# Full-array and paired-head products in the mixers of a hybrid encoder step

## The chip, the cores and the metric

The kernel runs on one core of a Trainium2 chip. The metric is the device time of one launch in microseconds, as the median of repeated runs. Five engines work side by side, each with its own in-order queue: TensorE (PE, matrix products; its weight loads are listed as PEld), VectorE (DVE), ScalarE (ACT), GpSimd (POOL) and SyncE (SP, which here only issues DMAs). A scheduler (the Tile framework) fixes the order of each queue when the program is built.

## What is computed

One layer of a streaming encoder, for a prompt of 2048 tokens and a sample chunk of 64 tokens with a past of 2048. Model width is 1024, and four mixers have four heads of 64 columns each.

```
proj = x @ w_in                                  # split among the mixers
A gated delta rule, chunks of c tokens, state S (64 x 64 per head):
   lm  = strictly lower part of (beta k) k^T * decay
   sol = (I + lm)^-1 [beta v, beta k exp(g)];  v_new = u - w S
   o   = (q exp(g)) S + (q k^T * decay) v_new;  S = S exp(g_last) + (k decay)^T v_new
B stick-breaking attention: z = q k^T / 8, weights from log-sigmoids and a running sum over keys
C mLSTM: o = (a_prev q C + (q k^T * D) v) / den;  C, n = decayed + (w k)^T [v, 1]
D HGRN2: a[t,s] = sum_k q[t,k] k[s,k] exp(l[t,k] - l[s,k]);  o = (q exp(l)) S + a v;  S likewise
o = rmsnorm per head, gates;  x = LN(alpha x + o @ w_out);  x = LN(alpha x + relu(x @ w1 + b1)^2 @ w2 + b2)
```

## The kernel before

The prompt is cut into 16 tiles of 128 tokens, two tiles make a unit (8 units, and one more for the 64 sample tokens), four tiles make a block (4 blocks). For each block the program projects the tokens, runs the attention over all key tiles up to the block, and then runs the mixers unit by unit: `gates`, `gdn`, `mlstm`, `hgrn`. The output product (`mix`) and the MLP of a block follow later in the program. The scheduler interleaves all of it: between the small products of the mixers, TensorE's queue holds products of the projections and of the MLP.

The large products (L413 to L415, L466) split each operand into a high and a low part in float32r and add three products; they use all 128 rows and 128 columns of the array. Their weights come through a ring of buffers `whi` and `wlo` (W_SP of each), loaded by DMAs that SP issues in order with all others (`move`, L192). The mixers' products are plain float32. A float32 product is issued as two instructions, so the counts of a row are twice the number of calls; a transpose is one.

An operand that occupies only part of the partitions makes a product on a part of the array. In the profile a row says so by two numbers, rows*columns: `128*128` is the full array, `64*128` uses 64 rows (partitions of the operands), `128*64` fills 64 columns (partitions of the result).

The places that the change touches:

- `attention`, L1197 to L1205: for each key tile and head a score product of keys (high part in one half of the partitions, low part in the other, `kk`) with the high part of the queries `qs` over 128 rows (L1204), then a second one of the 64 rows of the keys' high part with the queries' low part `ql` (L1205). There are 160 such pairs: four blocks, four heads, 4, 8, 12 and 16 key tiles. L1163/L1164 and L1211/L1212 are the attention's other products, on the full array.
- `gdn`, the inverse of the delta rule's matrix: the loop over the unit's tiles `j` at L872 inverts one tile's matrix after the other, by products on 64 x 64 parts of the array (L889, L894, L906, L911) and transposes (L900), each waiting for a copy on ScalarE or a subtraction on VectorE. Then L924/L925 multiply by the inverse: for each head, first a 64*64 product for the upper half, then a 128*64 one for the lower half.
- State updates, L937 (delta rule), L1007 (mLSTM), L1132 (HGRN2): for each head a product with 64 columns, into the half of the partitions that the head has in the state.
- `mlstm`, L982 to L986: the scores of the heads 0 and 2, then those of 1 and 3, each over the 64 rows of that half, through one PSUM buffer (ring `h`, one bank).
- `hgrn`, L1088 to L1112: for each head products of 32 columns at five levels (L1105, 64*32), and of 64 and 32 columns (L1100, 64*64 and 64*32), then copies on ScalarE and a multiplication and a reduction on VectorE, again through the one bank of ring `h`.
- The buffer rings at the head of the file (L25 to L36).

Of the kernel before, what the change touches and what calls it, by code (L numbers as in the profile page):

```python
# [13 lines left out]
P = 128  # L14
# [10 lines left out]
W_RAW, W_SP = 4, 7  # L25
R_X2 = 7
MIX_AT = (8, 12)
R_AS, R_AR, R_AQ, R_AK, R_OB = 4, 4, 2, 4, 1
# [7 lines left out]
R_G2, R_G1, R_H2, R_H1 = 7, 12, 2, 12  # L36
# [17 lines left out]
def encoder_step(ctx: ExitStack, tc: tile.TileContext, a, o):  # L54
# [139 lines left out]
    def rows(i):  # L194
        return slice(64 * i, 64 * i + 64)
# [567 lines left out]
    def gdn(u):  # L763
# [102 lines left out]
        for j in range(n):  # L866
            for d, s in ((sq.wd[j], wb), (sq.wtd[j], tb)):
                for h in range(4):
                    r0 = (j * 4 + h) * NB
                    SP.dma_start(diag(d, h, half), s[r0 : r0 + NB])  # L870
        for j in range(n):
            c, t = ch[j], u.tiles[j]  # L872
            sl = slice(j * C, (j + 1) * C)
            c.W, c.WT = g1([C, 4, half]), g1([C, 4, half])
            for d, dst in ((sq.wd[j], c.W), (sq.wtd[j], c.WT)):
                for x in range(2):
                    d0 = x * (half * 4 * half + half)
                    SP.dma_start(dst[x * half : x * half + half], d[d0 : d0 + half * 4 * half].rearrange("(r h c) -> r h c", r=half, h=4))

            bs = 16  # L880
            while 2 * bs < C:
                cu, yt = g1([C, 4, half]), g1([C, 4, half])
                for x in (A, B):
                    m0 = x.start % 64
                    POOL.tensor_tensor(cu[x], c.U[x, :, x], bmask[bs][x, m0 : m0 + half].unsqueeze(1).to_broadcast([half, 4, half]), ALU.mult)
                py = ps([C, 4, half])
                for h in range(4):
                    for x in (A, B):
                        PE.matmul(py[x, h, :], lhsT=cu[x, h, :], rhs=c.WT[x, h, :], start=True, stop=True)  # L889
                ACT.copy(yt, py)  # L890
                p1 = ps([C, 4, half])
                for h in range(4):
                    for x in (A, B):
                        PE.matmul(p1[x, h, :], lhsT=yt[x, h, :], rhs=c.W[x, h, :], start=True, stop=True)  # L894
                DVE.tensor_tensor(c.W, c.W, p1, ALU.subtract)

                m = C if 4 * bs < C else half
                p2 = ps([half, 4, m])
                for h in range(4):
                    PE.transpose(p2[:, h, :], c.W[:m, h, :], ident[:m, :m])  # L900
                for x in (A, B)[: m // half]:
                    ACT.copy(c.WT[x], p2[:, :, x])
                bs *= 2
            py = ps([C, 4, half])
            for h in range(4):
                PE.matmul(py[B, h, :], lhsT=c.U[A, h, B], rhs=c.WT[A, h, :], start=True, stop=True)  # L906
            yt = g1([C, 4, half])
            ACT.copy(yt[B], py[B])
            p1 = ps([half, 4, half])
            for h in range(4):  # L910
                PE.matmul(p1[:, h, :], lhsT=yt[B, h, :], rhs=c.W[B, h, :], start=True, stop=True)  # L911
            c.WB = g1([C, 4, half])
            POOL.tensor_copy(c.WB[B], c.W[B])
            ACT.mul(c.WB[A], p1, -1.0)

# [19 lines left out]
            sd = ps([P, 2, 64])  # L935
            for h in range(4):
                PE.matmul(sd[rows(h % 2), h // 2, :], lhsT=c.kd[:, h, :], rhs=vn[:, h, :], start=True, stop=True)  # L937
            for h in range(4):
                r = rows(h % 2)
                DVE.scalar_tensor_tensor(S[r, h // 2, r], S[r, h // 2, r], c.dec[r, h // 2 : h // 2 + 1], sd[r, h // 2, :], ALU.mult, ALU.add)  # L940
# [8 lines left out]
    def mlstm(u):  # L949
        C, n, N, b, sq = u.C, u.n, u.N, u.b, u.seq  # L950
        Cn = sq.Cn
        for j in range(n):
            t = u.tiles[j]
            q = h1([P, 2, C])
            SP.dma_start(q, b.mlq[:, :, t.off : t.off + C].rearrange("g p t -> p g t"))
            k = h1([C, 4, 64])
# [48 lines left out]
            sd = ph([P, 2, 65])  # L1005
            for h in range(4):
                PE.matmul(sd[rows(h % 2), h // 2, :], lhsT=kw[:, h, :], rhs=v[:, h, :], start=True, stop=True)  # L1007
            for h in range(4):
                i = h % 2
                r = rows(i)  # L1010
                cs = Cn[r, h // 2, 65 * i : 65 * i + 65]
                DVE.scalar_tensor_tensor(cs, cs, app[r, h // 2, C - 1 : C], sd[r, h // 2, :], ALU.mult, ALU.add)


    def hgrn(u):
# [10 lines left out]
        for t in u.tiles:  # L1026
# [61 lines left out]
            for g in range(2):  # L1088
# [480 lines left out]
```

## Time and profile before

| what | value |
|---|---|
| time, median of 3 runs | 3481.16 us (3478.19 to 3486.56) |
| time of the profiled execution | 3476.89 us |
| span of its instructions | 3475.2 us |
| TensorE busy | 3298.9 us, 95% |
| VectorE busy | 2265.2 us, 65% |
| ScalarE, GpSimd busy | 1376.5 us (40%), 850.8 us (24%) |
| mean granted TensorE clock | 0.957 |

The page gives busy time by engine, the span in 40 slices, the chain of work that ended last, and the costliest groups of instructions. A timeline row gives the start in us, the length, engine, line, operation, what it writes and reads, and a count where neighbours are merged. Lengths of products overlap, since they are pipelined: what a product costs the queue is the distance from its start to the start of the next one.

### The profile page before, as it was taken

What the parts mean: (1) busy time and instruction counts of PE and PEld (TensorE: products, weight loads), DVE (VectorE), ACT (ScalarE), POOL (GpSimd) and SP (SyncE); (2) the same over time, 40 slices, a digit from 0 to 9 for tenths busy, and PEclk for the clock granted to TensorE, in tenths of its full rate; (3) what the DMA queues carried; (4) which work ended last, traced back from release to release, by engine and by line L of the source; (5) the groups of instructions that cost most, each with busy time, mean ns of one, the idle gap of its engine ahead of it and who ended that gap; (6) DMA issues with size and microseconds to landing.
All of it is one profiled execution on the core that took longest, in us unless ns stands there. A gap on an engine that the chain in (4) does not pass through costs nothing.

```text
span 3475.2 us, 61244 instructions
## 1 busy us (share of the span) xinstructions
PE 3298.9 (95%) x21186; PEld 2702.3 (78%) x21186; DVE 2265.2 (65%) x5524; ACT 1376.5 (40%) x3308; POOL 850.8 (24%) x907
## 2 busy tenths in 40 slices
PE   7988999899989999999999999999999999999997
PEld 7987787878776777777677767777777778798986
DVE  2327647547767897669968985797686354564445
ACT  2224434434545455555555544445242111121111
POOL 4322212211124234443525322133021000010001
PEclk9998898899988998999999989999999999999999
DMA  7995665466565786668769555574866587675552
GB/s 226 306 328 170 188 194 189 140 209 186 182 194 192 255 273 218 217 228 256 250 197 308 185 175 161 183 243 146 286 210 208 164 291 234 230 227 164 164 163 77
DMA packets 575313, 731.44 MB, mean 210 GB/s; under 512 B 104680, under 2 KB 305308, under 8 KB 575004
## 3 DMA queue, kind: packets, MB, share of 16 engines
q1 hardware_dynamic: 575004, 727.53, 65.0%
q8 instruction: 168, 2.75, 0.3%
q14 instruction: 141, 1.16, 0.1%
HBM read 544.37 MB, written 182.94 MB: 209 GB/s over the span
## 4 chain that ended last, share of the span: by engine, by line
PE 59%; DVE 12%; DMA 5%; issue 2%; SPq 1%; ACT 1%; POOL 1%; POOLq 0%; DVEq 0%; ACTq 0%
PE d L413 16%; PE d L415 15%; PE d L414 15%; PE a L1205 1%; PE d L466 1%; PE po L1212 1%; PE po L1211 1%; PE a L1164 1%; DVE acc L1426 1%; PE a L1163 1%; DMA vv<-x 1%; PE a L1204 1%; DMA x<-x1d 1%; PE h L1105 1%; DVE ar L1169 1%
## 5 line engine op out<-in xcount | busy, mean ns | idle before, releaser
L413 PE MATMUL d<-XH,whi 128*128 128x512 f32 (+1 forms) x1840 | 666.1, 363 | 9.4 <-ACT whi L405 4.0
L414 PE MATMUL d<-XL,whi 128*128 128x512 f32 (+1 forms) x1840 | 665.4, 362 | 2.0 <-DVE XL L429 2.0
L415 PE MATMUL d<-XH,wlo 128*128 128x512 f32 (+1 forms) x1840 | 660.8, 360 | 0.3 <-POOL wlo L406 0.3
L1426 DVE TENSOR_TENSOR acc<-d,acc 128x512 f32<-128x512 f32 x564 | 385.0, 687 | 188.0 <-PE d L415 177.2
L413 PE MATMUL d<-whi,hh 128*128 128x512 f32 x992 | 403.6, 407 | 11.3 <-DVE acc L1426 9.5
L1161 POOL TENSOR_TENSOR ar<-as,ar 128x512 fp32r<-128x512 f32 (+3 forms) x177 | 208.9, 1180 | 786.5 <-ACT ar L1160 675.0
L415 PE MATMUL d<-whi,hh 128*128 128x512 f32 x992 | 397.0, 400 | 0.0
L413 PEld LDWEIGHTS d<-XH,whi 128*128 128x128 f32 x1840 | 349.7, 190 | 60.0 <-ACT whi L405 4.2
L414 PE MATMUL d<-wlo,hh 128*128 128x512 f32 x992 | 395.5, 399 | 0.0
L414 PEld LDWEIGHTS d<-XL,whi 128*128 128x128 f32 x1840 | 349.6, 190 | 52.1 <-issue 3.4
L415 PEld LDWEIGHTS d<-XH,wlo 128*128 128x128 f32 x1840 | 349.7, 190 | 49.0 <-issue 2.3
L406 POOL TENSOR_TENSOR wlo<-raw,whi 128x512 fp32r<-128x512 f32 (+1 forms) x204 | 276.8, 1364 | 334.1 <-ACT whi L405 198.6
L413 PE MATMUL d<-whi,XH 128*128 128x256 f32 (+1 forms) x1024 | 295.2, 296 | 5.9 <-DVE x L528 4.3
L414 PE MATMUL d<-wlo,XH 128*128 128x256 f32 (+1 forms) x1024 | 298.4, 293 | 1.1 <-DMA wlo<-wsp 1.1
L415 PE MATMUL d<-whi,XL 128*128 128x256 f32 (+1 forms) x1024 | 297.8, 293 | 0.0
L1405 ACT ACTIVATE x<-d,cbig 128x512 f32<-128x512 f32 (+1 forms) x160 | 97.8, 611 | 474.3 <-PE d L415 466.9
L1407 DVE CAST hh<-x 128x512 fp32r<-128x512 f32 (+1 forms) x160 | 80.2, 501 | 255.3 <-ACT x L1406 254.9
L413 PEld LDWEIGHTS d<-whi,hh 128*128 128x128 f32 x992 | 188.9, 190 | 58.3 <-DVE acc L1426 11.9
L415 PEld LDWEIGHTS d<-whi,hh 128*128 128x128 f32 x992 | 188.7, 190 | 45.6 <-issue 1.9
L414 PEld LDWEIGHTS d<-wlo,hh 128*128 128x128 f32 x992 | 189.1, 191 | 40.8 <-issue 0.5
L413 PEld LDWEIGHTS d<-whi,XH 128*128 128x128 f32 x1024 | 198.2, 197 | 10.3 <-ACT whi L405 4.5
L414 PEld LDWEIGHTS d<-wlo,XH 128*128 128x128 f32 x1024 | 201.2, 197 | 5.0 <-DMA wlo<-wsp 1.8
(444 smaller groups left out, 6542.7 us busy)
## 6 DMA issues: line engine op xcount, KB each, us to landing
whi<-wsp SPq DMA_DIRECT2D x644, 256.0 KB
wlo<-wsp SPq DMA_DIRECT2D x644, 256.0 KB
wsp<-whi SPq DMA_DIRECT2D x196, 256.0 KB
wsp<-wlo SPq DMA_DIRECT2D x196, 256.0 KB
raw<-in_w_dram SPq DMA_DIRECT2D x128, 256.0 KB
raw<-in_w_in_dram SPq DMA_DIRECT2D x52, 256.0 KB
ak<-kk SPq DMA_DIRECT2D x80, 128.0 KB
ak<-vv SPq DMA_DIRECT2D x80, 128.0 KB
```

Of the source, the lines that this page charges most:

```text
L406: POOL.tensor_tensor(lo, raw, hi.bitcast(F32), ALU.subtract)
L413: PE.matmul(out, lhsT=lh, rhs=rh, start=start, stop=False)
L414: PE.matmul(out, lhsT=lh, rhs=rl, start=False, stop=False)
L415: PE.matmul(out, lhsT=ll, rhs=rh, start=False, stop=stop)
L466: PE.matmul(pt, lhsT=lhs(k), rhs=r, start=k == ks[0] and i == 0, stop=k == ks[-1] and i == 1)
L1105: PE.matmul(pc[32 * qd : 32 * qd + 32, 32 * li : 32 * li + 32], lhsT=lh[r, ts_], rhs=rh[r, ts_], start=True, stop=True)
L1161: POOL.tensor_tensor(sl, sp, sh.bitcast(F32), ALU.subtract)
L1163: PE.matmul(c, lhsT=tri_, rhs=sh, start=True, stop=False)
L1164: PE.matmul(c, lhsT=tri_, rhs=sl, start=False, stop=True)
L1405: ACT.activation(r, pt, AF.Relu, bias=b1c(ff))
L1407: DVE.tensor_copy(h[:, f, cs], r)
L1426: lambda pt, first, acc=acc: DVE.tensor_tensor(acc, pt, acc, ALU.add),
```

## The change

Buffers are moved between the rings: W_SP 7 to 6, the staging ring `x2` 7 to 6, `aq` 2 to 3, `g2` 7 to 10, `g1` 12 to 9, `h2` 2 to 3.

- Attention: `ql` is loaded for each head into both halves of the partitions (two DMAs a head instead of one for two heads), and the second score product runs over 128 rows. It then also adds the product of the two low parts.
- Delta rule: both tiles' inverses are made side by side, each step for both tiles before the next step; one copy and one subtraction serve both. The inverse is put together in one array WF of 128 x 128 for each head (a memset and two copies on GpSimd, one scaling on ScalarE), and the product with it is one product of the full array for each head.
- mLSTM: a second copy of the queries `qw` with zeros in the other head's half (a memset on GpSimd, two DMAs) lets one product over 128 rows make the scores of two heads; one VectorE operation for all four heads.
- HGRN2: two heads share one PSUM bank; the products of 64 columns are cut into two of 32; copies, multiplication and reduction serve two heads.
- State updates: one product of the full array for two heads; of its result the two diagonal blocks are read.

```diff
-W_RAW, W_SP = 4, 7
-R_X2 = 7
+W_RAW, W_SP = 4, 6
+R_X2 = 6
...
-R_AS, R_AR, R_AQ, R_AK, R_OB = 4, 4, 2, 4, 1
+R_AS, R_AR, R_AQ, R_AK, R_OB = 4, 4, 3, 4, 1
...
-R_G2, R_G1, R_H2, R_H1 = 7, 12, 2, 12
+R_G2, R_G1, R_H2, R_H1 = 10, 9, 3, 12
...
+        while 2 * bs < C:
+            cu, yt = g2([C, n, 4, half]), g2([C, n, 4, half])
...
+            py = ps([C, n, 4, half])
+            for j in range(n):
+                for h in range(4):
+                    for x in (A, B):
+                        PE.matmul(py[x, j, h, :], lhsT=cu[x, j, h, :], rhs=WT[x, j, h, :], start=True, stop=True)
+            ACT.copy(yt, py)
...
+            DVE.tensor_tensor(W, W, p1, ALU.subtract)
...
+        for j in range(n):
+            WF = ch[j].WF = g2([C, 4, C])
+            POOL.memset(WF[B, :, A], 0.0)
+            POOL.tensor_copy(WF[A, :, A], W[A, j])
+            POOL.tensor_copy(WF[B, :, B], W[B, j])
+            ACT.mul(WF[A, :, B], p1[:, j], -1.0)
...
-                PE.matmul(pv[A, h, :], lhsT=c.W[A, h, :], rhs=R[A, h, :], start=True, stop=True)
-                PE.matmul(pv[B, h, :], lhsT=c.WB[:, h, :], rhs=R[:, h, :], start=True, stop=True)
+                PE.matmul(pv[:, h, :], lhsT=c.WF[:, h, :], rhs=R[:, h, :], start=True, stop=True)
...
-            sd = ps([P, 2, 64])
-            for h in range(4):
-                PE.matmul(sd[rows(h % 2), h // 2, :], lhsT=c.kd[:, h, :], rhs=vn[:, h, :], start=True, stop=True)
+            sd = ps([P, 2, P])
+            for g in range(2):
+                PE.matmul(sd[:, g, :], lhsT=pairs(c.kd)[:, g, :], rhs=pairs(vn)[:, g, :], start=True, stop=True)
...
+            qw = h2([P, 2, 2 * C]).rearrange("p g (i t) -> p g i t", i=2)
+            POOL.memset(qw, 0.0)
+            for i in range(2):
+                SP.dma_start(qw[rows(i), :, i, :], b.mlq[:, rows(i), t.off : t.off + C].rearrange("g p t -> p g t"))
...
-            for i in range(2):
-                r = rows(i)
-                pq = ph([C, 2, C])
-                for g in range(2):
-                    PE.matmul(pq[:, g, :], lhsT=kT[r, g, :], rhs=q[r, g, :], start=True, stop=True)
-                DVE.scalar_tensor_tensor(E[:, i::2, :], pq, 0.125, E[:, i::2, :], ALU.mult, ALU.mult)
+            pq = ph([C, 4, C])
+            for g in range(2):
+                PE.matmul(pq[:, 2 * g : 2 * g + 2, :], lhsT=kT[:, g, :], rhs=qw[:, g], start=True, stop=True)
+            DVE.scalar_tensor_tensor(E, pq, 0.125, E, ALU.mult, ALU.mult)
...
+            for i in range(2):
+                r = rows(i)
+                pc = ph([C, 2, 256])
+                for g in range(2):
...
+                            for c in range(0, x, 32):
+                                PE.matmul(pc[d0 + c : d0 + c + 32, g, 192 : 192 + x], lhsT=F[x][r, base + s0 + c : base + s0 + c + 32], rhs=F[x][r, base + s0 + x : base + s0 + 2 * x], start=True, stop=True)
...
+                mm = h2([C, 2, 160])
+                DVE.tensor_tensor(mm, pc[:, :, 0:160], hmask[:C].rearrange("p l t -> p (l t)").unsqueeze(1).to_broadcast([C, 2, 160]), ALU.mult)
+                DVE.tensor_reduce(acc[:, i::2, :], mm.rearrange("p g (l t) -> p g t l", l=5), axis=AX.X, op=ALU.add)
...
-            ql = aq([P, N], F32R)
-            move(ql, b.ql[g, :, 0:N])
...
-                qs = aq([P, N], F32R)
+                qs, ql = aq([P, N], F32R), aq([P, N], F32R)
                 for k in range(2):
                     move(qs[rows(k)], b.qh[g, r, 0:N])
+                    move(ql[rows(k)], b.ql[g, r, 0:N])
...
-                        PE.matmul(z, lhsT=kk[r, ks], rhs=ql[r, q0:N], start=False, stop=True)
+                        PE.matmul(z, lhsT=kk[:, ks], rhs=ql[:, q0:N], start=False, stop=True)
```

## Rows read from the trace of the kernel before

**Rows 1.** The page: busy time by engine, chain that ended last by engine.
```profile
PE 3298.9 (95%) x21186; PEld 2702.3 (78%) x21186; DVE 2265.2 (65%) x5524; ACT 1376.5 (40%) x3308; POOL 850.8 (24%) x907
...
PE 59%; DVE 12%; DMA 5%; issue 2%; SPq 1%; ACT 1%; POOL 1%; POOLq 0%; DVEq 0%; ACTq 0%
```

**Rows 2.** Windows of 100 us: busy us of each engine, granted clock, DMA.
```profile
900.00:1000.00 100.00, 86.48 (x521) 73.22 (x520) 74.68 (x230) 50.66 (x124) 19.23 (x22) 0.86 0.57 172
...
1200.00:1300.00 100.00, 91.44 (x495) 72.31 (x495) 97.03 (x230) 52.41 (x123) 37.30 (x33) 0.94 0.83 268
...
1400.00:1500.00 100.00, 100.00 (x553) 76.30 (x552) 57.52 (x101) 52.02 (x105) 47.42 (x42) 1.00 0.67 225
```

**Rows 3.** Lines with shapes kept apart, TensorE: count, busy us, mean ns, idle before.
```profile
L1205 PE MATMUL a<-aq,ak 64*128 64x512 f32 x112 | 58.0, 518 | 0.0
...
L1205 PE MATMUL a<-aq,ak 64*128 64x128 f32 x16 | 5.3, 333 | 0.0
```

**Rows 4.** Timeline of TensorE, one pair of score products.
```profile
2151.59 0.39 PE L413 MATMUL d<-whi,hh 128*128 128x512 f32 x1
2151.82 0.40 PE L1204 MATMUL a<-aq,ak 128*128 128x512 f32 x1
2152.15 0.50 PE L1205 MATMUL a<-aq,ak 64*128 64x512 f32 x1
2152.58 0.50 PE L414 MATMUL d<-wlo,hh 128*128 128x512 f32 x1
2152.91 0.39 PE L415 MATMUL d<-whi,hh 128*128 128x512 f32 x1
```

**Rows 5.** Timeline of TensorE, product with the inverse (delta rule).
```profile
1436.83 0.33 PE L924 MATMUL m<-g,g 64*64 64x64 f32 x2
1437.08 0.33 PE L925 MATMUL m<-g,g 128*64 128x64 f32 x2
...
1438.88 0.50 PE L414 MATMUL d<-wlo,hh 128*128 128x512 f32 x1
```

**Rows 6.** Timeline of TensorE, four float32 products of the full array (HGRN2).
```profile
2026.76 1.00 PE L1127 MATMUL h<-h,h 128*128 128x64 f32 x8
2027.57 0.48 PE L413 MATMUL d<-XH,whi 128*128 128x512 f32 x1
```

**Rows 7.** Timeline of TensorE, one head of HGRN2.
```profile
2622.66 0.48 PE L1100 MATMUL h<-h 64*64 64x64 f32 x4
2622.93 0.22 PE L1105 MATMUL h<-h 64*32 64x32 f32 x2
...
2623.44 0.51 PE L413 MATMUL d<-whi,hh 128*128 128x512 f32 x1
```

**Rows 8.** Timeline of TensorE: mLSTM scores, and two full-array passes of 256 columns.
```profile
1239.60 0.71 PE L985 MATMUL h<-h,h 64*128 64x128 f32 x4
1240.24 0.50 PE L1164 MATMUL a<-ar,XH 128*128 128x512 f32 x1
...
1251.36 0.59 PE L794 MATMUL m<-g,cbig 128*128 128x256 f32 x2
...
1252.03 0.40 PE L414 MATMUL d<-XL,whi 128*128 128x512 f32 x1
```

**Rows 9.** Timeline of TensorE: one step of an inverse.
```profile
2075.54 0.68 PE L894 MATMUL m<-g,g 64*64 64x64 f32 x16
2076.15 0.50 PE L415 MATMUL d<-XH,wlo 128*128 128x512 f32 x1
```

**Rows 10.** Timeline of TensorE: one state update.
```profile
1521.88 0.45 PE L937 MATMUL m<-g,g 128*64 128x64 f32 x8
1522.27 0.50 PE L415 MATMUL d<-XH,wlo 128*128 128x512 f32 x1
```

**Rows 11.** Waits: of TensorE for a weight, of SP's queue (us, times, longest).
```profile
PE d L413 <- ACT whi L405: 4.0, 1, 4.0
...
SPq L192 <- PE d L415: 710.0, 332, 13.1
```

More of the change, by code (lines that the diff above doesn't have):

```diff
@@ new lines, in gdn @@
+        py = ps([C, n, 4, half])
+        for j in range(n):
+            for h in range(4):
+                PE.matmul(py[B, j, h, :], lhsT=ch[j].U[A, h, B], rhs=WT[A, j, h, :], start=True, stop=True)
+        yt = g2([C, n, 4, half])
+        ACT.copy(yt[B], py[B])
+        p1 = ps([half, n, 4, half])
+        for j in range(n):
+            for h in range(4):
+                PE.matmul(p1[:, j, h, :], lhsT=yt[B, j, h, :], rhs=W[B, j, h, :], start=True, stop=True)
+        for j in range(n):
+            WF = ch[j].WF = g2([C, 4, C])
[3 more added lines that the diff above has]
+            ACT.mul(WF[A, :, B], p1[:, j], -1.0)
@@ L873, in gdn @@
             sl = slice(j * C, (j + 1) * C)
[L874 to L886, printed above, removed]
-                for h in range(4):
[L888 to L914, printed above, removed]
             pk = ps([C, 4, 64])
@@ L934, in gdn @@
             ACT.copy(og, po.rearrange("p h d -> p (h d)"))
-            sd = ps([P, 2, 64])
-            for h in range(4):
-                PE.matmul(sd[rows(h % 2), h // 2, :], lhsT=c.kd[:, h, :], rhs=vn[:, h, :], start=True, stop=True)
+            sd = ps([P, 2, P])
+            for g in range(2):
+                PE.matmul(sd[:, g, :], lhsT=pairs(c.kd)[:, g, :], rhs=pairs(vn)[:, g, :], start=True, stop=True)
             for h in range(4):
                 r = rows(h % 2)
-                DVE.scalar_tensor_tensor(S[r, h // 2, r], S[r, h // 2, r], c.dec[r, h // 2 : h // 2 + 1], sd[r, h // 2, :], ALU.mult, ALU.add)
+                DVE.scalar_tensor_tensor(S[r, h // 2, r], S[r, h // 2, r], c.dec[r, h // 2 : h // 2 + 1], sd[r, h // 2, r], ALU.mult, ALU.add)
             SP.dma_start(gt, t.ga[:, 0:256])
@@ L1004, in mlstm @@
             POOL.tensor_tensor(kw, k, bc(ws, [C, 4, 64]), ALU.mult)
-            sd = ph([P, 2, 65])
-            for h in range(4):
-                PE.matmul(sd[rows(h % 2), h // 2, :], lhsT=kw[:, h, :], rhs=v[:, h, :], start=True, stop=True)
+            sd = ph([P, 2, 130])
+            for g in range(2):
+                PE.matmul(sd[:, g, :], lhsT=pairs(kw)[:, g, :], rhs=pairs(v)[:, g, :], start=True, stop=True)
             for h in range(4):
@@ L1010, in mlstm @@
                 r = rows(i)
[L1011 to L1012 removed]
+                ic = slice(65 * i, 65 * i + 65)
+                cs = Cn[r, h // 2, ic]
+                DVE.scalar_tensor_tensor(cs, cs, app[r, h // 2, C - 1 : C], sd[r, h // 2, ic], ALU.mult, ALU.add)
     def hgrn(u):
@@ L1087, in hgrn @@
             acc = view(lc[:C], [C, 4, 32])
-            for g in range(2):
-                base = g * C
-                for i in range(2):
-                    r = rows(i)
-                    h = 2 * g + i
-                    pc = ph([C, 256])
+            for i in range(2):
+                r = rows(i)
+                pc = ph([C, 2, 256])
+                for g in range(2):
+                    base = g * C
                     for x in (64, 32):
@@ L1129, in hgrn @@
             ACT.copy(og, po.rearrange("p h d -> p (h d)"))
-            sd = ph([P, 2, 64])
-            for h in range(4):
-                PE.matmul(sd[rows(h % 2), h // 2, :], lhsT=kn[:, h, :], rhs=v[:, h, :], start=True, stop=True)
+            sd = ph([P, 2, P])
+            for g in range(2):
+                PE.matmul(sd[:, g, :], lhsT=pairs(kn)[:, g, :], rhs=pairs(v)[:, g, :], start=True, stop=True)
             for h in range(4):
                 r = rows(h % 2)
-                DVE.scalar_tensor_tensor(H[r, h // 2, r], H[r, h // 2, r], dec[r, h // 2 : h // 2 + 1], sd[r, h // 2, :], ALU.mult, ALU.add)
+                DVE.scalar_tensor_tensor(H[r, h // 2, r], H[r, h // 2, r], dec[r, h // 2 : h // 2 + 1], sd[r, h // 2, r], ALU.mult, ALU.add)
             SP.dma_start(gt, t.hgg)
```

37 lines of the change are left out of this document (28 added, 9 removed).

## Prediction, made before the changed kernel was run

> **What bounds the kernel now.** I read the page first: TensorE is busy for 95% of the span, no other engine for more than 65%, and the chain that ended last runs through TensorE for 59% and through VectorE for 12% [rows 1]. So the kernel is as long as TensorE's queue, plus its holes (3475.2 - 3298.9 = 176 us). Then the windows of 100 us: the reader is to see two kinds of stretch. In one TensorE is busy all the time, as in 1400 to 1500; in the other it has holes, and VectorE is at 97% (1200 to 1300) or the granted clock fell to 0.86 (900 to 1000) [rows 2]. From 300 to 2700 us, where the mixers run, ten of the 24 windows have TensorE busy for 97 us or more, fourteen for less. Last, the timeline, because "busy" hides what a product costs the queue: that is the distance between starts.
>
> A full-array product of 512 columns costs 0.23 us (L413 to L1204, 2151.59 to 2151.82). Around the second score product, over 64 rows, three distances grow: L1204 to L1205 is 0.33, L1205 to the next 0.43, and the first full product after it has 0.33 before its follower [rows 4]. Nothing is waited for: L1205 has no idle time before it [rows 3]. So going to a part of the array costs some 0.10 us, coming back another 0.10 on the first full product, and this 64-row product itself 0.20 more than a full one. The same 0.33 us stand on both sides of other small products. The change is about these costs: it takes small-tile products out of the queue or puts more of them into one visit.
>
> **Part by part.** I write the fixed price of a visit as 0.20 us (0.10 in, 0.10 out) and add the run from its first start to the first full product.
>
> *Attention scores.* One pair costs 0.33 + 0.43 + 0.33 = 1.09 us for three products that would cost 3 x 0.23 = 0.70 on the full array: 0.39 less. 160 pairs, 112 of them 512 wide and 48 narrower [rows 3, 4]; I take 0.39 for all: 62 us. Where the neighbour in the queue is another small product, the exit remains; for an estimated sixth of them I leave only 0.20: 57 us. Bounds: 32 (0.20 for all) and 64. The extra DMAs (24 more) and the third buffer of `aq` lie beside other work: SP waited 710 us just for weight buffers to come free, so it has room [rows 11].
>
> By a rule of the Trainium skill this would go the other way ("TensorEngine Tiling (Array Packing)", Theoretical Speedup): a contraction of 64 rows gives up to a factor of 2, since two row tiles work at the same time. By it the change would give something away (the rival on concurrency). The trace does not bear it out here: the L1205 of the row stands alone between full-array products and costs more than one, not half.
>
> *Product with the inverse.* L924 and L925 alternate between two tile shapes, eight switches within one call: 1438.88 - 1436.83 = 2.05, with the visit 2.25 us [rows 5]. Afterwards it is four float32 products of 64 columns on the full array, the shape of L1127: 0.81 and some 0.1 on the exit, 0.9 us [rows 6]. 16 x 1.35 = 22 us.
>
> *HGRN2.* One head is 2623.44 - 2622.66 = 0.78, with the visit 0.98; of it 0.27 are the first four instructions with the change from 64*64 to 64*32 [rows 7]. Cut into 32 columns these become some of the cheap ones: 40 and more instructions fill the other 0.51, 12 ns each, so 0.06. Two heads in one visit: 2 x (0.51 + 0.06) + 0.20 = 1.34 against 1.96; 32 pairs give 20 us. Bounds: 13 (the switch alone) and 28 (a head that is now broken into two visits, as some are).
>
> *mLSTM scores.* Two visits of 0.64 + 0.20 = 1.68; four full passes of 256 columns cost twice (1252.03 - 1251.36 - 0.23) = 0.88 [rows 8]. 16 x 0.8 = 13 us.
>
> *Inverses side by side.* A step is 0.61 + 0.20 = 0.81 [rows 9]. Of two steps in one visit at least 0.20 is saved, at most some 0.36 (the start of the run is shared too). Seven such visits a unit (L889, L894 and L906, L911, L900's second), 8 units: 56 x 0.2 to 0.36 is 11 to 20; I take 15.
>
> *State updates.* 0.39 + 0.20 = 0.59 now [rows 10], afterwards four passes of 128 columns, half of the 0.44 of two passes of 256 each [rows 8], 0.44: 48 x 0.15 = 7 us. This is the part with the least in it, because eight column-tile instructions run nearly on top of each other.
>
> Demand on TensorE falls by 57 + 22 + 20 + 13 + 15 + 7 = 134 us (bounds 95 and 155).
>
> *What is added elsewhere.* GpSimd gets the memsets of `qw` and WF and two copies, at 24% busy [rows 1]; ScalarE and VectorE get fewer and larger operations. If GpSimd were late, `wlo` of a new weight would wait behind a memset. I cost that at nothing.
>
> *Rings.* One buffer less for `whi`/`wlo`. SP issues loads in order and waits for those buffers 332 times; TensorE itself waited once, 4.0 us, for a scaled weight [rows 11]. One buffer is held for twelve products, 12 x 0.23 = 2.8 us, so up to 2.8 us of lead go. In the steps of the projection with four weight loads (six in each block, 24) a load could come up to 1 us late: bounds 0 and 25 us, I take 5, near the single wait of now. `g1` at 9 can hold back the next unit's convolution; the mixers have slack, as TensorE is full after them anyway.
>
> **From demand to time.** A us taken from TensorE's queue is a us of span only where TensorE is the bound. By the windows about half of the saving (67) lies in full ones and counts whole. The other half lies in windows with holes, 13.5 and 8.6 us in the two shown, where VectorE or a latency sets the pace between bursts [rows 2]; there I count 0.6: 40 us. 67 + 40 - 5 = 102, say 100. Against the profiled execution, 3476.9 - 100 = 3377; that one lies 4 us below the median of the runs shown, so **3380 us**.
>
> **Rivals.**
> *The bound passes to VectorE and to latencies* (20%). For: 97% in 1200 to 1300. Then the half in windows with holes gives nothing, and holes that grow bring the low clock with them (13.5 us of hole at 0.86 [rows 2]): 134 / 2 - 5 - 10 = 52, 3429 us. Against: VectorE is at 65% over the span, and it is relieved as well.
> *Holes close too* (13%). HGRN2 and mLSTM turn their one PSUM bank half as often, the two inverses' latencies run beside each other. If a quarter of the 176 us of holes go and all of the demand counts: 134 + 44 = 178 less in the best case; I set 150, 3330 us.
> *Weights come late* (5%): slower than before. With one buffer less, each of the 328 groups of weight loads (in each of four blocks 6 and 12 in the projection, 16 in the output product, 16 and 32 in the MLP) finds SP, which issues in order, blocked. From 100 / 328 = 0.3 us a group the gain is gone; at 0.4 us it is 3510 us. Against: one such wait of 4.0 us now [rows 11].
> *The shape is not the cause* (4%): the 0.10 us would belong to small operands, not to the switch, and a second score product over 128 rows would stay at 0.43. Then attention, the biggest term, falls away, and with it a part of the others: some 30 us, 3450 us. Against: L1163/L1164 and all full products on the same buffers keep 0.23.
>
> *Concurrency is lost* (2%): a narrow product leaves the rest of the array to its neighbour, as the eight instructions of a state update do, which start within 0.39 us [rows 10]. If the second score product did so too, its full form would add half a product, 160 x 0.12 = 19 us, instead of taking 57; state updates would save nothing. 134 - 57 - 19 - 7 = 51, three quarters of it on the path, less 5: 33 us, 3448 us. Against: the 0.43 us behind L1205 [rows 4]. The Trainium skill's page named above is what would speak for it.
>
> **How the numbers follow.** Forecast 3380 with 56% (own range 3350 to 3410); the rivals as above. Leaving out the slower case, the two at 3448 and 3450 us and part of the tails of "bound passes" and "holes close", 8 in 10 lie between 3315 and 3445. A measurement of this kernel can tell 0.2% (7 us) from no change. Faster by more: 92%; within: 3%; slower: 5%.
>
> **What would show it.** Right: L1204 to the second score product 0.23 us and no 64*128 row of that line; the product with the inverse in under 1 us, without 64*64 rows; HGRN2 in two visits a tile, without 64*64 rows; TensorE's busy time lower by some 100 us while its share stays near 95%. Wrong: TensorE's waits for `whi` or `wlo` in tens of us (weights late); TensorE's share at 92% or less with VectorE over 95% in more windows (bound passed on); score products still 0.4 us apart (shape not the cause).

## The result, and the profile after

The changed kernel takes 3441.08 us (median of 4 runs, 3429.37 to 3448.17) against 3480.78 us: a ratio of 0.988, with a 95% interval of 0.985 to 0.991. It is 40 us faster; 100 were forecast. The profiled execution took 3441.77 us.

The page of after, span and busy time by engine:

```profile
span 3440.1 us, 60484 instructions
...
PE 3193.1 (93%) x20906; PEld 2687.6 (78%) x20906; DVE 2248.2 (65%) x5423; ACT 1355.5 (39%) x3186; POOL 868.0 (25%) x958
```

TensorE's busy time fell by 106 us [rows 1], and its holes grew from 176 to 247 us. So the work went, and most of its time stayed as waiting. The same three windows, and two others of 24, in the view of windows:

```profile
900.00:1000.00 100.00, 86.42 (x868) 74.41 (x867) 81.14 (x234) 50.37 (x132) 27.94 (x36) 0.90 0.57 170
1100.00:1200.00 100.00, 84.96 (x447) 69.58 (x448) 97.08 (x236) 49.33 (x117) 37.25 (x30) 0.93 0.69 221
1200.00:1300.00 100.00, 88.57 (x695) 71.89 (x694) 93.65 (x232) 50.20 (x120) 32.29 (x35) 0.91 0.82 263
1400.00:1500.00 100.00, 91.32 (x421) 71.91 (x421) 87.20 (x191) 55.00 (x126) 44.86 (x40) 1.00 0.72 232
...
2200.00:2300.00 100.00, 100.00 (x702) 81.05 (x701) 59.26 (x118) 49.49 (x109) 18.90 (x24) 1.00 0.61 192
```

The window 1400 to 1500, full before, now has 8.7 us of holes [rows 2]. From 300 to 2700 us ten windows had TensorE busy for 97 us or more; now four have, only two of them among the ten, and the holes of these 2400 us went from 117 to 188 us.

The windows do not hold the same products, though. A line of the delta rule before (L932) and after (L942), in the view by source line:

```profile
L932 PE MATMUL m<-g,g x136: 218/275/275, 447.2 to 2810.7; 128*128 128x64 f32 x128, 64*64 64x64 f32 x8
...
L942 PE MATMUL m<-g,g x136: 218/275/421, 450.0 to 2564.8; 128*128 128x64 f32 x128, 64*64 64x64 f32 x8
```

Its last product, all but the last of the mixers, starts 246 us earlier than before, while the whole is only 35 us shorter: of the 12822 large products (L413 to L415, L466) 8566 instead of 9461 now stand ahead of it in TensorE's queue, and the others behind. The growth of the holes lies almost all ahead of that point (154 to 222 us; behind it 23 and 25).

The products themselves, TensorE's timeline of after (score pair, product with the inverse, a step of two inverses, a state update):

```profile
2155.03 0.39 PE L1217 MATMUL a<-aq,ak 128*128 128x512 f32 x1
2155.26 0.40 PE L1218 MATMUL a<-aq,ak 128*128 128x512 f32 x1
2155.49 0.39 PE L1178 MATMUL a<-ar,XH 128*128 128x512 f32 x1
...
1408.62 1.00 PE L935 MATMUL m<-g,g 128*128 128x64 f32 x8
1409.43 0.47 PE L413 MATMUL d<-XH,whi 128*128 128x512 f32 x1
1409.74 0.39 PE L414 MATMUL d<-XL,whi 128*128 128x512 f32 x1
...
1943.14 1.15 PE L896 MATMUL m<-g,g 64*64 64x64 f32 x32
1944.22 0.44 PE L1134 MATMUL h<-cbig,h 128*128 128x128 f32 x2
...
2101.42 0.39 PE L414 MATMUL d<-wlo,hh 128*128 128x512 f32 x1
2101.66 0.61 PE L1020 MATMUL h<-h,h 128*128 128x130 f32 x4
2102.02 0.48 PE L415 MATMUL d<-whi,hh 128*128 128x512 f32 x1
2102.34 0.39 PE L413 MATMUL d<-whi,hh 128*128 128x512 f32 x1
```

Both score products stand 0.23 us from their followers (0.33 and 0.43 before [rows 4]). The product with the inverse takes 0.81 us and 0.08 on the exit (2.25 before [rows 5]). HGRN2 is different:

```profile
1842.88 0.25 PE L1119 MATMUL h<-h 64*32 64x32 f32 x6
1843.06 0.33 PE L1177 MATMUL a<-ar,XH 128*128 128x128 f32 x1
...
1843.61 0.31 PE L1119 MATMUL h<-h 64*32 64x32 f32 x10
1843.84 0.33 PE L1178 MATMUL a<-ar,XH 128*128 128x128 f32 x1
1844.10 0.26 PE L1119 MATMUL h<-h 64*32 64x32 f32 x6
1844.29 0.50 PE L413 MATMUL d<-whi,oh 128*128 128x512 f32 x1
...
1845.86 0.26 PE L1119 MATMUL h<-h 64*32 64x32 f32 x8
```

The products of two heads, meant as one visit, are queued in pieces, with attention's and dense products between them. Counted as unbroken stretches of the trace, L1114 and L1119 make 121 visits for 34 pairs of heads. But L1100 and L1105 had been in pieces too: 175 visits for 68 heads.

TensorE's waits, the rows of the kernel before that stand against those below (us, times, longest):

```profile
PE po L1212 <- DVE ar L1169: 10.0, 10, 3.3
PE po L1211 <- ACT ar L1168: 9.9, 7, 2.0
```

and of after, with SP's queue in the last row:

```profile
PE po L1224 <- ACT ar L1182: 26.8, 17, 5.8
PE po L1225 <- DVE ar L1183: 17.2, 17, 2.2
PE d L413 <- DVE as L1172: 14.1, 8, 5.3
PE d L413 <- DMA whi<-wsp: 13.1, 5, 6.1
...
PE a L1177 <- ACT ar L1174: 12.5, 9, 3.3
...
SPq L192 <- PE d L415: 635.4, 313, 11.8
```

The largest growth is at `po`, the product of attention's weights with the values: 20 us before, 44 after. Such a wait in the timeline (in brackets the idle time and what ended it):

```profile
1442.09 0.39 PE L413 MATMUL d<-XH,whi 128*128 128x512 f32 x1
1442.32 0.40 PE L1177 MATMUL a<-ar,XH 128*128 128x512 f32 x1
1443.80 0.51 PE L1225 MATMUL po<-ar,ak 128*128 128x512 f32 x1 [1.08 <-DVE ar L1183]
1444.14 0.39 PE L414 MATMUL d<-XL,whi 128*128 128x512 f32 x1
1444.38 0.40 PE L415 MATMUL d<-XH,wlo 128*128 128x512 f32 x1
```

L414 and L415 behind it belong to the projection that was running at 1442.09, yet they start only after `po`: the queue was fixed when the program was built.

### The profile page after: what moved, and what is told of

It reads as the page before. It is cut to its first block, busy times and chain, and to the rows that moved or that the text cites. A ratio compares the mean times of both kernels' runs of the same rounds, so it can differ in the third digit from the quotient of the medians.

```text
span 3440.1 us, 60484 instructions
## 1 busy us (share of the span) xinstructions
PE 3193.1 (93%) x20906; PEld 2687.6 (78%) x20906; DVE 2248.2 (65%) x5423; ACT 1355.5 (39%) x3186; POOL 868.0 (25%) x958
## 5 line engine op out<-in xcount | busy, mean ns | idle before, releaser
L413 PE MATMUL d<-XH,whi 128*128 128x512 f32 (+1 forms) x1840 | 666.5, 363 | 11.2 <-DMA whi<-wsp 4.0
L415 PE MATMUL d<-XH,wlo 128*128 128x512 f32 (+1 forms) x1840 | 661.8, 360 | 2.0 <-POOL wlo L406 1.6
L414 PE MATMUL d<-XL,whi 128*128 128x512 f32 (+1 forms) x1840 | 663.0, 360 | 0.1
L413 PE MATMUL d<-whi,hh 128*128 128x512 f32 x992 | 402.6, 407 | 20.0 <-DVE as L1172 6.6
L413 PEld LDWEIGHTS d<-XH,whi 128*128 128x128 f32 x1840 | 351.0, 191 | 61.1 <-DMA whi<-wsp 4.3
L415 PE MATMUL d<-whi,hh 128*128 128x512 f32 x992 | 397.0, 400 | 0.0
L414 PE MATMUL d<-wlo,hh 128*128 128x512 f32 x992 | 395.9, 399 | 0.4 <-DMA wlo<-wsp 0.4
L415 PEld LDWEIGHTS d<-XH,wlo 128*128 128x128 f32 x1840 | 351.1, 191 | 51.4 <-POOL wlo L406 2.3
L414 PEld LDWEIGHTS d<-XL,whi 128*128 128x128 f32 x1840 | 350.8, 191 | 47.0 <-DVE XL L429 0.4
L413 PE MATMUL d<-whi,XH 128*128 128x256 f32 (+1 forms) x1024 | 296.8, 298 | 20.7 <-DMA whi<-wsp 7.8
L414 PE MATMUL d<-wlo,XH 128*128 128x256 f32 (+1 forms) x1024 | 298.1, 294 | 5.3 <-POOL wlo L406 4.6
L415 PE MATMUL d<-whi,XL 128*128 128x256 f32 (+1 forms) x1024 | 297.2, 293 | 0.0
L413 PEld LDWEIGHTS d<-whi,hh 128*128 128x128 f32 x992 | 188.8, 190 | 69.3 <-DVE as L1172 8.2
L415 PEld LDWEIGHTS d<-whi,hh 128*128 128x128 f32 x992 | 189.2, 191 | 43.8
L414 PEld LDWEIGHTS d<-wlo,hh 128*128 128x128 f32 x992 | 189.6, 191 | 41.9 <-DMA wlo<-wsp 0.8
L413 PEld LDWEIGHTS d<-whi,XH 128*128 128x128 f32 x1024 | 198.1, 197 | 26.5 <-DMA whi<-wsp 8.5
L414 PEld LDWEIGHTS d<-wlo,XH 128*128 128x128 f32 x1024 | 201.1, 197 | 8.3 <-POOL wlo L406 5.2
```

The costliest lines, as they stand in the source:

```text
L413: PE.matmul(out, lhsT=lh, rhs=rh, start=start, stop=False)
L414: PE.matmul(out, lhsT=lh, rhs=rl, start=False, stop=False)
L415: PE.matmul(out, lhsT=ll, rhs=rh, start=False, stop=stop)
```

## Experiments

A table is needed to read them. The span of a profiled execution is split into three: *work*, TensorE's busy time with the part at the lower granted level (1.2 GHz) counted half (a product of 512 columns lasts 0.39 us at one level and 0.79 at the other); *clock*, the other half of that part; *holes*, span less busy time. "Shapes" counts neighbours in TensorE's queue that use different parts of the array (rows and columns taken as 32, 64 or 128). us is the median of the timed runs, and all else is from one profiled execution of each kernel. The kernel before took 3481 to 3487 us beside the other runs; the ratios below, with 95% intervals, are against its runs on the same chip.

| kernel | us | span | work | clock | holes | shapes |
|---|---|---|---|---|---|---|
| before | 3480.8 | 3475 | 3179 | 120 | 176 | 1439 |
| e1 before, small rings | 3516.9 | 3519 | 3189 | 114 | 216 | 1424 |
| e3 = e1 + scores | 3471.7 | 3473 | 3138 | 110 | 224 | 1105 |
| e5 before, W_SP 6, x2 6 | 3478.6 | 3470 | 3183 | 110 | 177 | 1412 |
| e9 = e5 + scores | 3479.8 | 3479 | 3132 | 121 | 226 | 1102 |
| e15 = e5, one unit swapped | 3504.4 | 3502 | 3182 | 137 | 183 | 1443 |
| e16 = e15 + scores | 3468.5 | 3462 | 3132 | 124 | 206 | 1137 |
| e13 = e5, all units swapped | 3534.4 | 3528 | 3191 | 124 | 214 | 1472 |
| e14 = e13 + scores | 3500.8 | 3492 | 3143 | 132 | 217 | 1194 |
| e10 before + scores, updates | 3461.0 | 3464 | 3123 | 131 | 210 | 1022 |
| e11 = e10 + grouping | 3448.8 | 3448 | 3108 | 124 | 216 | 921 |
| after | 3441.1 | 3440 | 3079 | 114 | 247 | 649 |
| e2 after, small rings | 3443.8 | 3445 | 3069 | 126 | 251 | 588 |
| e4 = e2 - scores | 3484.7 | 3487 | 3124 | 141 | 222 | 905 |
| e12 = e2, G1 12 | 3444.0 | 3446 | 3064 | 122 | 259 | 588 |
| e18 = e2, last unit swapped | 3504.3 | 3499 | 3090 | 143 | 266 | 677 |
| e17 = e2, all units swapped | 3475.8 | 3472 | 3082 | 138 | 252 | 713 |
| e7 after, VectorE relieved | 3445.7 | 3440 | 3078 | 108 | 255 | 621 |
| e6 after, W_SP 5 | 3513.7 | 3528 | 3078 | 174 | 276 | 689 |
| e8 = e6, inverses in turn | 3475.4 | 3469 | 3089 | 128 | 252 | 710 |

**The score products and the staging rings (e1 to e4).** The whole change taken apart at equal, smaller staging rings; e3 adds to e1, and e4 takes from e2, one line (excerpts).

```diff
-W_RAW, W_SP = 4, 7        # e1; e2 sets 3 and 5 in the changed kernel
-R_X2 = 7
+W_RAW, W_SP = 3, 7
+R_X2 = 5
-    PE.matmul(z, lhsT=kk[r, ks], rhs=ql[r, q0:N], ...)   # e3; e4 the reverse
+    PE.matmul(z, lhsT=kk[:, ks], rhs=ql[:, q0:N], ...)
```

> The kernel before with smaller staging rings alone (raw weights 4 to 3, x2 7 to 5), as a base for the next runs, which need the memory. Theory 'holes come from speed' (TensorE's queue, relieved of its switch costs, now waits at places where it used to come late): within 10 us of before. Theory 'rings' (smaller rings make TensorE wait, and that ate the gain): 20 us or more slower than before, with TensorE's holes up by as much.

> The changed kernel with the same smaller staging rings (raw 3, x2 5; its whi/wlo ring stays at 6). Holes from speed: within 10 us of the changed kernel, 3441 us, so some 40 us below e1. Rings: 15 us or more slower than the changed kernel.

> e1 with one line changed: the second score product runs over all 128 rows (the other half meets the low part of the keys with the other head's queries, a term too small to be seen). Nothing else moves: no DMA, no buffer. Demand on TensorE falls by 160 x 0.39 = 62 us. Holes from speed: TensorE's busy time and switch costs fall by 55 to 62 us, its holes rise by 20 to 40, and the time falls by 20 to 35 us against e1. Rings: holes stay, the time falls by 45 us or more.

> e2 with the second score product put back to 64 rows (loads and buffers as in the changed kernel). Holes from speed: 20 to 35 us slower than e2, with fewer holes. Rings: 45 us or more slower than e2.

Ratios to before: e1 1.0092 [1.0076, 1.0108], e2 0.9879 [0.9858, 0.9901], e3 0.9957 [0.9941, 0.9973], e4 1.0007 [0.9993, 1.0022]. The one line is worth 51 to 55 us of work, as forecast (57), and here 45 and 41 us of time. Smaller rings cost the kernel before 32 us and the changed one 3. By the expectations e1 and e3 speak for the rings (though e3's holes grew by 8), e2 speaks against them, and e4 falls between the two. After these four runs it looked as if relief of TensorE counts for 0.8 and the rings had taken the rest; the next runs took that apart.

**The rings of the change (e5, e6), and VectorE (e7).** Excerpts:

```diff
-W_RAW, W_SP = 4, 7        # e5, on before
-R_X2 = 7
+W_RAW, W_SP = 4, 6
+R_X2 = 6
-W_RAW, W_SP = 4, 6        # e6, on after
+W_RAW, W_SP = 4, 5
-    DVE.tensor_tensor(al, zc, ah.bitcast(F32), ALU.subtract)   # e7, on after, W_RAW 3
-    return ah, al, c[0:1, :]
+    return ah, ah, c[0:1, :]
```

> The kernel before with the two ring cuts of the change that it can hold: whi/wlo 7 to 6, x2 7 to 6, nothing else. Theory 'rings' (the change's own cuts of the rings cost TensorE holes that hid part of the gain): 25 to 35 us slower than before, TensorE's holes up by 25 to 40 us, its busy time as before. Theory 'holes from speed': within 8 us of before.

> The changed kernel with one more whi/wlo buffer taken away, 6 to 5. Rings: 20 us or more slower than the changed kernel, with more waits of TensorE for whi and wlo. Holes from speed: within 8 us.

> The changed kernel (raw ring 3 instead of 4) with the attention's low part of the weights left out: VectorE's subtraction is gone (177 of them, some 0.6 us each, about 105 us of VectorE's time), and TensorE multiplies the high part twice, so its work is unchanged. The output lacks that low part. Theory 'VectorE is the bound between full stretches': 25 us or more faster than the changed kernel. Theory 'latency and order' (TensorE waits for the end of single chains, not for a full engine): 5 to 17 us faster, the waits for that subtraction alone (17 us now). Rings alone: no change.

e5: 0.9981 [0.9967, 0.9994], no loss by W_SP 6 and x2 6 together. e6: 1.0100 [1.0074, 1.0126]. e7 leaves out the low part of attention's weights, and multiplies the high part twice in its place, so that only VectorE is relieved. 0.9894 [0.9877, 0.9911]; its page:

```profile
PE 3185.3 (93%) x20906; PEld 2686.4 (78%) x20906; DVE 2144.5 (62%) x5246; ACT 1353.0 (39%) x3186; POOL 850.9 (25%) x958
```

VectorE lost 104 us of work and the time did not move (3445.66 against 3441.08); 25 us or more had been expected if its capacity were the bound. The edit also gives the queues another order, worth tens of us by the runs further down, so the time alone does not settle it. The holes say more: 255 us, within the 247 to 266 of the changed kernel in its other orders. So nothing here shows VectorE's capacity as the bound, in spite of windows at 97%.

**Inverses one after the other (e8).** e6 with the loop over `j` outermost again (excerpt):

```diff
-        while 2 * bs < C:
-            for j in range(n):
+        for j in range(n):
+            bs = 16
+            while 2 * bs < C:
```

> e6 with the two inverses of a unit made one after the other again, each step with its own copy and subtraction; the full-array product with the inverse stays. Demand on TensorE rises by some 15 us. Theory 'denser mixers' (the shorter chain of a unit packs the work of VectorE and ScalarE more tightly, and the holes come from there): the mixers end 100 to 200 us later, holes fall, and the time is within 8 us of e6 or lower. Without that: 10 to 15 us slower than e6.

0.9976 [0.9961, 0.9992]: 38 us faster than e6, though its work is 11 us more. The 11 us are near the 15 forecast for side by side, but an order alone moves the work by as much (e18, below). Time and holes fell as the theory of denser mixers said, but the sign that it named for itself did not come: the product of L942 (here L933) ends at 2609 us against 2619 in e6, and not 100 to 200 us later. Something else moves the time by tens of us.

**Parts at the large rings (e9 to e11), and G1 (e12).** e9 is the line of e3 on e5. e10 adds to before, with its own rings, that line and the state updates; e11 also cuts HGRN2's 64-column products and groups the product with the inverse (excerpt):

```diff
+            for h in range(4):
                 PE.matmul(pv[A, h, :], lhsT=c.W[A, h, :], ...)
+            for h in range(4):
                 PE.matmul(pv[B, h, :], lhsT=c.WB[:, h, :], ...)
...
-R_G2, R_G1, R_H2, R_H1 = 10, 9, 3, 12      # e12, on e2
+R_G2, R_G1, R_H2, R_H1 = 10, 12, 3, 12
```

> The kernel before with the rings of e5_before_w6_x6 (W_SP 6, R_X2 6; 3478.58 us) and the one line of e3_before_full_scores: the second score product contracts over 128 rows. TensorE's busy time should fall by about 51 as there. Theory (TensorE runs its queue in a planned order, and about 0.8 of a first relief of this size becomes time wherever the rings are large enough): 3478.6 - 0.8 x 51 = 3438, which is already the time of the whole change. Rival (the small rings of e1 made the score products' relief worth more than it is with large rings): 3460 or more. Rival (the full relief converts): 3428.

> The kernel before with its own rings (W_SP 7, R_X2 7, W_RAW 4), the score line and the full-array state updates, and nothing else of the change. The demand on TensorE should fall by 51 for the scores and by some 6 to 8 for 48 updates. Theory (0.8 of a relief of this size): 3481 - 0.8 x 58 = 3435. Rival (conversion ends at about 40 us whatever is taken away, since the waits of the attention chain are then next): 3440, with holes that grew by all the rest. Rival (small): 3460.

> The kernel before with its own rings, score line, state updates, the 64-column HGRN2 products cut into 32-column ones so that all products of a head have one shape, and the product with the inverse in two groups of four (all four 64-row products, then all four full ones) in place of alternating. No product of two heads together, no inverses side by side, and no other buffers. Demand: scores 51, updates 7, product with the inverse 16 x 1.35 = 22 as forecast, HGRN2 5 to 10 by the cut alone: about 87. Theory (0.5 to 0.8 of it becomes time, the share falling with the amount): 3481 - 44..70 = 3411 to 3437, so faster than or equal to the changed kernel (3441), which takes away 105 but pays for denser rings. Rival (all that lies beyond some 40 us goes to waits, whichever products are relieved): 3440. Rival (the product order in the delta rule delays the units): above 3450.

> The changed kernel with the staging rings of e2_after_small_rings (W_RAW 3, R_X2 5; 3443.81 us) and the ring G1 of the delta rule back from 9 to the 12 of before. If the shorter ring is where the relief went (its owners wait for buffers), the time falls by 10 or more, to 3430 or below, and the holes with mixers as releaser fall from 40 to 50 us. If the ring is idle slack, 3438 to 3450 and the holes stay near 247.

e9: 0.9983 [0.9971, 0.9995]. The line that was worth 45 us in e3 is worth nothing here: 51 us of work gone, 49 of holes come. The waits of `po` in e5:

```profile
PE po L1211 <- ACT ar L1168: 12.4, 8, 6.4
...
PE po L1212 <- DVE ar L1169: 7.3, 9, 1.7
```

and in e9:

```profile
PE po L1211 <- ACT ar L1168: 17.3, 13, 4.1
PE po L1212 <- DVE ar L1169: 16.9, 15, 3.3
```

e10: 0.9927 [0.9904, 0.9951], 56 us of work for 24 of time. e11: 0.9895 [0.9879, 0.9912], 71 for 37. Both theories asked for more (3435; 3411 to 3437). e12: 0.9875 [0.9853, 0.9898]. In e12 TensorE's queue as built is row by row that of e2, and so is the time, 3443.99 against 3443.81: the shorter G1 costs nothing here. The two profiles of this one queue differ by 5 us in work and 8 in holes, so differences of that size in the table say nothing. In all the others the queue differs: of e3 against e1 from TensorE's instruction 6858 of 21186 on, of e9 against e5 from 2647.

**The order alone (e13, e15) and the line on top (e14, e16).** Two readings were left: the holes swallow relief at large rings, or each build draws another order, itself worth tens of us. So the order was changed and nothing else, and then the line was added to each.

```diff
         gdn(u)             # e13; e15 for the first unit alone
-        mlstm(u)
         hgrn(u)
+        mlstm(u)
```

> The kernel of e5_before_w6_x6 (3478.58 us) with nothing but the order in which a unit's mixers are written changed: HGRN2 ahead of mLSTM. The same instructions, the same demand on TensorE, the same rings; the order of the queues comes out otherwise. Theory A (the order that a build happens to get is worth tens of us, as e9_before_large_rings_scores against e3_before_full_scores hints): the time differs from 3478.6 by 10 to 40 us in either direction, TensorE's busy time by less than 15, and the difference is in the holes. Theory B (order hardly matters; each kernel's time follows from its demand and rings): 3470 to 3487.

> e13_before_other_order with the second score product over 128 rows, which takes 51 us from TensorE's queue. Theory A: the relief counts for 0.8 of itself on average, plus or minus the draw of the order: e13 - 41, within 20 us. Theory B' (with these larger rings the relief gives nothing, since waits of the attention chain take its place, as e9 showed against e5): within 10 us of e13.

> e5_before_w6_x6 with HGRN2 ahead of mLSTM in the first of the nine units alone: the smallest edit of the order. Theory A: still up to 20 us away from 3478.6, in the holes, since all that is queued later moves. Theory B: within 5 us.

> e15_before_one_unit_swapped with the second score product over 128 rows. Theory A: e15 - 41 within 20 us. Theory B': within 10 us of e15.

Ratios: e13 1.0149 [1.0119, 1.0180], e14 1.0059 [1.0037, 1.0081], e15 1.0058 [1.0037, 1.0078], e16 0.9954 [0.9939, 0.9969]. The same computation with two mixers of one unit exchanged is 26 us slower; in all units, 56. The pages of e5:

```profile
span 3469.8 us, 61357 instructions
...
PE 3292.8 (95%) x21186; PEld 2697.7 (78%) x21186; DVE 2257.4 (65%) x5524; ACT 1380.3 (40%) x3308; POOL 840.7 (24%) x907
```

and of e15, as many products on TensorE, 26 us longer busy:

```profile
span 3501.9 us, 61331 instructions
...
PE 3318.6 (95%) x21186; PEld 2710.7 (77%) x21186; DVE 2251.6 (64%) x5524; ACT 1380.5 (39%) x3308; POOL 844.7 (24%) x907
```

By the table those 26 us are the lower granted clock (110 to 137), the work being the same; in e13 it is mostly holes. The line is worth 36 us in e16 and 34 in e14. Theory A holds in kind but was too small: e13 moved by 56 us (10 to 40 expected) and e15 by 26 (up to 20), and in e15 the difference is in the clock and not in the holes. That relief gives nothing at large rings falls.

**The order alone, in the changed kernel (e17, e18).** The same exchange on e2: all units, and the sample's unit alone.

> The changed kernel with the rings of e2_after_small_rings (3443.81 us) and HGRN2 ahead of mLSTM in every unit, as e13 did to the kernel before (there +56 us). If the order that a build gets is worth as much in the changed kernel, the time differs from 3444 by 10 to 60 us, more likely upward; if the changed kernel has so many waits already that its order no longer matters, 3436 to 3452. Either way TensorE's busy time stays near 3194.

> e2_after_small_rings with HGRN2 ahead of mLSTM in the sample's unit alone. Order matters: up to 25 us away from 3444, as e15 was from e5 by one unit; order does not matter: within 6 us.

e17: 0.9970 [0.9959, 0.9981], 32 us slower than e2. e18: 1.0052 [1.0032, 1.0073], 60 us slower than e2, by one unit of nine (up to 25 expected). The page of e18:

```profile
span 3499.3 us, 60522 instructions
...
PE 3232.8 (92%) x20906; PEld 2714.5 (78%) x20906; DVE 2256.2 (64%) x5423; ACT 1355.6 (39%) x3186; POOL 869.5 (25%) x958
```

Against e2 it has work +21 (89 more changes of shape: visits broken up), clock +17, holes +15.

**What the orders say together.** Means of three orders each (work, clock, holes):

| | us, three orders | mean | work | clock | holes |
|---|---|---|---|---|---|
| before (e5, e15, e13) | 3478.6, 3504.4, 3534.4 | 3506 | 3185 | 124 | 191 |
| + scores (e9, e16, e14) | 3479.8, 3468.5, 3500.8 | 3483 | 3136 | 126 | 216 |
| whole change (e2, e18, e17) | 3443.8, 3504.3, 3475.8 | 3475 | 3080 | 136 | 256 |

The whole change has staging rings one smaller than the others here. Two things are apart now. Holes grow by over half of what the work falls: +25 for -49, +65 for -105. For the whole change this lies outside the scatter (holes 177 to 214 before, 251 to 266 after), and the smaller staging rings are not what does it: the changed kernel with its own rings has 247, the kernel before with the smaller ones (e1) 216. For the scores alone it does not (206 to 226). Around that, a draw of the order moves a kernel by up to 60 us. From three orders each, the gain of the whole change is 3506 - 3475 = 31 us, give or take some 24 (the standard deviation within a three is about 29; over the root of three it is 17 for each mean, 24 for the difference); the 40 us of the two kernels as they stand are one pair of draws. So the gain over orders is little more than its own uncertainty.

## Why the prediction was wrong

**What bounds the kernel.** Half right. TensorE's queue and its holes do add up to the span. But a window at 100% was read as one in which TensorE is the bound and a us saved counts whole. Ten of 24 windows were full before and four after the change; in e9 four, in e5 eight. A reading that fits, though no run isolates it: full meant only that the order had just enough dense products in front of each wait.

**Demand, part by part.** Work fell by 100 us (3179 to 3079) against 134 (bounds 95 to 155). The scores (51 to 55 for 57) are right, three other steps by their rows: the product with the inverse 0.89 us for 0.9; a state update 0.36 + 0.09 = 0.45 for 0.44; a step of two inverses 1.08 us to its follower, one visit, for two of 0.61 [rows 9]. HGRN2's step "two heads in one visit" took it that products written together are queued together, and they came in pieces; but so had the heads before, and the visits fell from 175 to 121, by more than was forecast. Of the seven visits a unit to be merged, that of the transposes (L903) was not: they are still issued for each tile.

All six parts can be priced in the traces, by the distances between the starts of TensorE's products (holes taken off, low clock counted half, entry and exit beside products of 512 columns included), as means of four orders each (before, e5, e13, e15; after, e2, e17, e18):

| part | forecast, us | measured, us |
|---|---|---|
| scores | 57 | 48 |
| product with the inverse | 22 | 21 |
| HGRN2 | 20 | 17 |
| mLSTM scores | 13 | 11 |
| inverses side by side | 15 | 10 |
| state updates | 7 | 2 |

The sum is 109 of 134, within the bounds of 95 to 155, and not where the prediction failed. Every part but the state updates came to two thirds of its forecast or more. Over all 51 state updates the mean went from 0.53 to 0.49 us; the 0.59 worked out from one row [rows 10] and taken for all was too high.

The Trainium skill ("TensorEngine Tiling (Array Packing)", Theoretical Speedup) would have given something away with 64 rows made 128; here the trace decides against it, since the 128-row product stands 0.23 us from its follower, the 64-row one stood 0.43.

**From demand to time.** This is the step that failed: "67 in full windows count whole, the other half 0.6", 0.75 together. That about half of the saving lies in full windows was right (by the starts of the products concerned 0.46 of it, in the windows with 97 us or more); the worth of a us, there and elsewhere, was not. The kernels as they stand converted 40 of 100; means over orders 28 of 105 in span (3500 to 3472), and for the scores alone 22 of 49; the rest came back as holes (71 us more in the kernels as they stand, 65 in the means) and, within the scatter, as lower clock (12 in the means). What comes late next, in the changed kernel: attention's chain (`po` waiting 44 us for 20), the weights (13.1 us in five waits on `whi`, which has no row of that size before), together 37 of the 71 us. In e2, with holes of 251, `po` waits 29.5 us only, so which waits take the relief hangs on the order as well. The prediction asked "is TensorE full" and not "how far ahead of its next wait does it run".

That the queue's order is fixed, so that relief only makes TensorE reach the same waits earlier, is read from the timeline at 1443.80 and not shown by an experiment. The nearest to one are the first stretches of three pairs, in which TensorE's queue is the same and only the scores differ: up to instruction 6857 (e1, e3), 8438 (e15, e16) and 8988 (e13, e14) the work falls by 16, 19 and 22 us, the holes grow by 10, 7 and 7, and the time changes by +2, -16 and -12 us. That fits, but e12, with e2's queue and nothing relieved, also differs from e2 by 5 us more holes and 7 less work over a stretch as long. A rival stands beside it: the changed kernel's queue holds some 600 to 900 fewer large products ahead of the mixers' end (the last product of L932, L942) in three of its four orders (8566 against 9143 to 9497 before; 8885 in e2), so less work lies there to fill the waits. No run tells the two apart, and the cause of the holes stays open. The Trainium skill ("PSUM — Partial Sum Buffer", Engine vs sequencer instructions) says that products start and complete in program order; the rows shown of full-array products agree, small products next to each other do not always: in e2 118 of 20906 instructions, all of HGRN2, start elsewhere in the order than the queue has them (rows in the last section).

**The rings.** 5 us, bounds 0 to 25: e5 bears out about nothing on the work of before, with any price inside the scatter of orders. What W_SP 5 cost in e6 (73 us), and the 32 of e1, cannot be told from such a draw; both stay open. TensorE's waits on `whi` are 19.3 us in e6 for 13.1 in the changed kernel, so only 6 of the 73 us show there.

**The rivals.** By number "concurrency is lost" (3448) and "the shape is not the cause" (3450) came nearest, by luck: both fall with the score pair at 0.23 us; only that the state updates would save nothing is near the 2 us found. By mechanism "the bound passes to VectorE and to latencies" (3429) came nearest. Its growing holes are what the means over orders show (the clock too, 124 to 136, but within the scatter); its VectorE half is not borne out by e7. "Holes close too" is the opposite of what happened. "Weights come late" is seen in size (13.1 us), not as a loss of the gain.

**A cause that was missing.** No term stood for the new order that any edit brings. A range for this kernel needs some 30 us on either side for it, whatever the sum says. The wide range (8 in 10 between 3315 and 3445) held the time at its upper end, the forecast's own (3350 to 3410) did not; with the last unit swapped (e18, 3504) the wide one would have missed as well, so that it held is in part luck.

No version that beats the changed kernel was found; e2 and e12 are equal to it within their intervals.

## What to carry to other kernels

Where a scheduler fixes the queues, price a relief of the fullest engine against the waits it will reach sooner, and take under half of it for time until an experiment says more. Before a difference of 1% is put down to an edit, change only the order (exchange two independent steps) and see how far the time moves. Operations written side by side are not queued side by side: count the visits in the trace, before the change as well as after.

## What the runs showed of the hardware

The exit price of 0.08 to 0.10 us is also paid after full-array float32 products: L415 behind L1020 has 0.32 before its follower in place of 0.23, and so has L413 behind L935 (0.31). The entry is free there (L414 to L1020 0.24), while it cost 0.10 into the 64-row product [rows 4]. So an exit is paid after a part of the array and after these full float32 products alike, an entry only, in these rows, into the part.

With the same products, the granted clock moved between 0.960 (e5) and 0.954 (e15) by the order alone, worth 27 us of busy time in these two profiles (over all their runs 0.955 to 0.961 against 0.951 to 0.955).

Small products on different parts of the array need not start in the order of the queue. e12 and e2 have the same queue: four instructions of L1114, then eight of L1119. e12 runs them so:

```profile
583.25 0.25 PE L1114 MATMUL h<-h 64*32 64x32 f32 x4 [0.47 <-DVE h L1088]
583.38 0.26 PE L1119 MATMUL h<-h 64*32 64x32 f32 x8
```

and e2 starts two of L1119 some 0.03 us ahead of two of L1114:

```profile
580.82 0.22 PE L1114 MATMUL h<-h 64*32 64x32 f32 x2
580.84 0.22 PE L1119 MATMUL h<-h 64*32 64x32 f32 x2
580.87 0.20 PE L1114 MATMUL h<-h 64*32 64x32 f32 x2
580.89 0.25 PE L1119 MATMUL h<-h 64*32 64x32 f32 x6
```
